# Feed-forward's first product by seven half products (Strassen) in place of eight for 20 of 22 pairs of tiles; adaLN's pace 0.2 for 0.25

## The chip, the cores and the metric

The kernel runs on one core of a Trainium2 chip. The metric is the device time of one execution in microseconds (us), as the median of three runs. The engines are named as in the profile: PE multiplies matrices (PEld is its weight load), DVE is the vector engine, ACT the scalar engine, POOL the GpSimd engine, and SP issues the loads.

## The reference

Two layers of a trunk run for 512 latent and 128 context tokens, 640 tokens in all, with weights shared between both groups. What matters here is the second half of each layer and the modulation vectors that it needs:

```python
def _adaln(cvec, w, b):
    m = jnp.dot(jax.nn.silu(cvec), w) + b          # w: 1024 x 6144
    return jnp.split(m, 6, axis=-1)

def _swiglu(h, w1, w2):                             # h: 640 x 1024
    a = jnp.dot(h, w1)                              # w1: 1024 x 5632
    gt, up = jnp.split(a, 2, axis=-1)
    return jnp.dot(jax.nn.silu(gt) * up, w2)        # w2: 2816 x 1024

# in each of the two layers, after the four mixers and their merge
xp = xp + gt2 * _swiglu(_modulate(_rmsnorm(xp, norm2_g[l]), sh2, sc2), w_ffn_in[l], w_ffn_out[l])
xs = xs + gt2 * _swiglu(_modulate(_rmsnorm(xs, norm2_g[l]), sh2, sc2), w_ffn_in[l], w_ffn_out[l])
```

## The kernel before

Every product is made in three passes: each fp32 operand x is held as a rounded part hi and a rest lo = x - hi, and `mm3` (L406 to L408) adds hi by hi, hi by lo and lo by hi in PSUM. A weight tile of 128 x 1024 values is loaded in one transfer of 512 KB into one of two `raw` buffers; `wload` then copies each half of 512 columns to `whi` on ACT (L394) and subtracts on DVE to get `wlo` (L395). There are five `whi` and five `wlo` buffers of 512 columns in turn, so a half can be made up to five halves ahead. These instructions carry a high priority for the scheduler (`WPRI`), and so do the evacuations (`EPRI`).

The normalised activations stand as `hT`, eight k-tiles of hi and lo for 640 tokens. Feed-forward's first product runs over 22 pairs j of weight tiles, a gate tile and an up tile of 128 columns of w1. Each tile takes 8 k-tiles x 3 passes for two groups of tokens, 256 and 384 (`GROUPS`): 48 matmuls a tile, 96 a pair. The gate's PSUM goes through Silu on ACT (L1768), DVE multiplies the up's PSUM by it (L1771), and `split` (L443 on ACT, L444 on DVE) makes hi and lo of the result. The pairs come in groups of 6, 6, 6 and 4 (`FF_SPLIT`), and after each group the second product adds its share to the residual: 20 tiles of 256 columns a group, `t` on DVE (L1623) and the addition to `big` on POOL for three quarters of them (L1624). The activations of the groups stand in turn in the buffers `kv` and `m` with `q`.

Beside this runs adaLN in the background (`adaln_all`), in slices of 512 columns: per step one tile `wm` of w_mod is loaded, DVE adds its product with the one vector into `msum0` (L471, a SCALAR_TENSOR_TENSOR), and ACT (L465) and POOL (L467) do the same for the other into `mtmp` and `msum1`. Eight steps make a slice; PE then transposes the sums (L478) and DVE reduces them (L479). `tick()` is called once per stretch of matmuls, and each call adds `BGRATE` steps. At four places of a layer `bg_until` emits what is still missing.

The Tile scheduler decides the order in which each engine's instructions stand, by its own estimate of when operands are ready. On the chip each engine then works through its list in that order.

Of the kernel before, what the change touches and what calls it, by code (L numbers as in the profile page):

```python
# [78 lines left out]
FF_SPLIT = (6, 6, 6, 4)  # L79

WPRI = 20000
EPRI = 500
DEFER = 2
BGRATE = 0.25
W3 = 1
# [136 lines left out]
def trunk(ctx: ExitStack, tc: tile.TileContext, a: dict, depth: int):  # L222
# [103 lines left out]
    ofs = Slots("of", 4, NTOK)  # L326
    raw_ring = ring("raw", 2, [P, 1088])
    hi_ring = ring("whi", 5, [P, 544], F32R)
# [154 lines left out]
    def adaln_all(items):  # L483
# [9 lines left out]
        for i, (l, ch) in enumerate(items):  # L493
# [6 lines left out]
            if (ch // 2) % 3 == 2:  # L500
# [5 lines left out]
                yield True  # L506
                ps = acc()
                T.transpose(ps[:8, :P], gcol, ident)
# [1176 lines left out]
    def mixers(l, d, *start):  # L1685
# [30 lines left out]
        drive(bulk, streams)  # L1716

    def layer(l, *start):
        d = {"of": {}, "m": [], "mg": []}
# [25 lines left out]
        if l + 1 < depth:  # L1745
            smalls(l + 1)
        j0 = 0
        for g, cnt in enumerate(FF_SPLIT):
            acts = []

            def fo(n, bufs=None):
                return sum((wload(l, ("fo", g, n, k), bufs=bufs) for k in range(0, cnt, 4)), [])
            for jx in range(cnt):
                j = j0 + jx
                if g == 3 and jx == 1:

                    extra = [ks.take(F32R) for _ in range(4)]
                    bufs = [(t[:, 0:512], t[:, 512:1024]) for t in extra]
                    pieces = {2: fo(2, bufs)}
                if g == 3 and jx == 2:  # L1760
                    pieces[3] = fo(3, bufs)
                pl = ks if g % 2 == 0 else (ms if jx < 4 else qs)
                sl = pl.take(F32R)
                at = r32(sl).rearrange("p (w n) -> p w n", w=2)
                sg = f640()

# [8 lines left out]
                for groups in (LATE, EARLY) if j == 0 else (GROUPS,):  # L1775
# [4 lines left out]
                    run(fm(wu, KT, hmov, cb, groups))  # L1780
                acts.append((at, pl, sl))
            if g == 0:
                gts = gate_rows(l, 1)
            if g == 3:
                if l + 1 < depth:
# [10 lines left out]
            else:  # L1796
                pieces = {0: fo(0), 1: fo(1), **pieces}
                hook = norm_tm(xs, pieces, cnt, lhs, gts, ks, 0 if l + 1 < depth else None)
                ks.give(*extra)
            for at, pl, sl in acts:  # L1800
# [9 lines left out]
    def final(x, ss, tt):  # L1810
        out = qs.take()
        qs.give(out)
        r = norm_r(ss)
# [87 lines left out]
```

## Time and profile before

| | |
|---|---|
| median of 3 runs | 2796.37 us (2795.75 to 2799.54) |
| profiled execution, its own time | 2797.74 us |
| its span | 2796.0 us |
| mean granted TensorE clock | 0.994 |
| PE busy | 2727.5 us, 98% of the span |
| DVE busy | 1853.6 us, 66% |
| ACT busy | 1352.5 us, 48% |
| POOL busy | 520.4 us, 19% |

A share of 98% means that PE is hardly ever without an instruction in flight; the shares of the others are means over stages that differ. Feed-forward runs from about 954 to 1420 us in the first layer and from about 2330 us to the end in the second.

### The profile page before, as it was taken

The page shows a single profiled execution, that of the slowest core. Times are in us where ns is not written, and L with a number is a line of the kernel's source. Part 1 is how long each engine was busy: PE and PEld are TensorE (multiplying, and loading weights), DVE is VectorE, ACT ScalarE, POOL GpSimd, SP SyncE. Part 2 cuts the span into 40 slices and gives each one's busy share as a digit, 9 for nine tenths or more (in the row PEclk, how much of TensorE's full clock was granted, in tenths as well). Part 3 has the DMA queues.
Part 4 walks back from the last instruction along what each step waited for, and adds up shares of the span by engine and source line. Part 5 has one row for each costly group of instructions (what it writes and reads, how often), then busy time and mean ns, then how long its engine had stood idle before and what let it go on. Part 6 is the DMA issues. An engine that isn't in the chain of part 4 may idle for free.

```text
span 2796.0 us, 51577 instructions
## 1 busy us (share of the span) xinstructions
PE 2727.5 (98%) x19946; PEld 2679.6 (96%) x19946; DVE 1853.6 (66%) x4412; ACT 1352.5 (48%) x3122; POOL 520.4 (19%) x506
## 2 busy tenths in 40 slices
PE   7999999999999999999989999999999999999998
PEld 4999999999999999999989989999999999999998
DVE  7786768888984746455587776888888445334344
ACT  5865446656653533233358654456666334222222
POOL 2010222120233404223150001211100221101012
PEclk9999999999999999999999999999999999999999
DMA  7233323121234324233332233211111232222221
GB/s 284 89 102 101 106 94 97 48 77 63 76 117 145 98 81 130 94 118 99 129 118 91 94 118 110 80 61 46 49 62 62 82 121 76 76 76 76 73 99 64
DMA packets 113206, 264.26 MB, mean 95 GB/s; under 512 B 13040, under 2 KB 38992, under 8 KB 112960
## 3 DMA queue, kind: packets, MB, share of 16 engines
q1 hardware_dynamic: 112960, 260.97, 28.6%
q8 instruction: 156, 2.56, 0.4%
q14 instruction: 90, 0.74, 0.1%
HBM read 252.73 MB, written 7.95 MB: 93 GB/s over the span
## 4 chain that ended last, share of the span: by engine, by line
PE 82%; DVE 9%; ACT 3%; issue 2%; DMA 2%; POOL 1%; SPq 0%; DVEq 0%; POOLq 0%; ACTq 0%
PE acc L406 23%; PE acc L407 23%; PE acc L408 23%; PE O L1216 2%; PE T L1206 2%; DVE msum L471 2%; DVE wlo L395 1%; DMA raw<-wflat 1%; PE S L1173 1%; DMA wm<-w_mod 1%; PE S L1174 1%; PE T L942 1%; ACT whi L394 1%; PE S L1473 0%; PE S L1182 0%
## 5 line engine op out<-in xcount | busy, mean ns | idle before, releaser
L406 PE MATMUL acc<-hT,whi 128*128 128x256 f32 (+1 forms) x3392 | 1053.9, 312 | 19.5 <-DVE hT L661 5.1
L407 PE MATMUL acc<-hT,whi 128*128 128x256 f32 (+1 forms) x3392 | 1054.3, 311 | 4.4 <-DVE hT L604 1.8
L408 PE MATMUL acc<-hT,wlo 128*128 128x256 f32 (+1 forms) x3392 | 1050.3, 310 | 0.1
L395 DVE TENSOR_TENSOR wlo<-raw,whi 128x512 fp32r<-128x512 f32 (+1 forms) x632 | 475.7, 757 | 366.0 <-ACT whi L394 363.6
L394 ACT CAST whi<-raw 128x512 fp32r<-128x512 f32 (+1 forms) x632 | 388.8, 620 | 626.8 <-PE acc L407 394.7
L406 PEld LDWEIGHTS acc<-hT,whi 128*128 128x128 f32 x3392 | 640.9, 189 | 26.7 <-DVE hT L661 5.9
L407 PEld LDWEIGHTS acc<-hT,whi 128*128 128x128 f32 x3392 | 642.2, 189 | 7.6 <-DVE hT L604 2.5
L408 PEld LDWEIGHTS acc<-hT,wlo 128*128 128x128 f32 x3392 | 641.3, 189 | 1.1 <-DVE wlo L395 0.4
L467 POOL TENSOR_TENSOR msum<-msum,mtmp 128x512 f32<-128x512 f32 x140 | 206.6, 1476 | 387.3 <-ACT msum L465 269.9
L1624 POOL TENSOR_TENSOR big<-big,t 128x256 f32<-128x256 f32 x150 | 125.6, 843 | 660.5 <-DVE t L1623 653.1
L1596 POOL TENSOR_TENSOR m<-m,f 128x256 f32<-128x256 f32 x96 | 98.0, 1023 | 558.0 <-DVE f L1594 343.7
L406 PE MATMUL acc<-whi,kv 128*128 128x256 f32 x660 | 183.8, 281 | 2.3 <-DVE t L1623 2.3
L408 PE MATMUL acc<-whi,kv 128*128 128x256 f32 x660 | 183.6, 281 | 0.0
L407 PE MATMUL acc<-wlo,kv 128*128 128x256 f32 x660 | 183.3, 281 | 0.0
L1623 DVE TENSOR_TENSOR t<-acc,P 128x256 f32<-128x256 f32 x200 | 83.7, 421 | 126.3 <-PE acc L408 108.0
L721 ACT CAST pth<-T 128x512 fp32r<-128x512 f32 (+1 forms) x232 | 117.9, 522 | 96.9 <-PE T L1206 38.2
L406 PE MATMUL acc<-big,whi 128*128 128x256 f32 (+1 forms) x512 | 158.9, 310 | 3.5 <-ACT f L1588 3.5
L465 ACT ACTIVATE mtmp<-wm,csil 128x512 f32<-128x512 f32 x140 | 101.1, 722 | 121.8 <-POOL msum L467 109.1
L407 PE MATMUL acc<-big,whi 128*128 128x256 f32 (+1 forms) x512 | 158.8, 310 | 0.0
L408 PE MATMUL acc<-big,wlo 128*128 128x256 f32 (+1 forms) x512 | 158.4, 310 | 0.0
L722 DVE TENSOR_TENSOR ptl<-T,pth 128x512 fp32r<-128x512 f32 (+1 forms) x232 | 137.4, 602 | 31.2 <-ACT pth L721 30.1
L471 DVE SCALAR_TENSOR_TENSOR msum<-wm,csil,msum 128x512 f32<-128x512 f32 x140 | 148.2, 1059 | 7.4 <-DMA wm<-w_mod 6.2
(400 smaller groups left out, 5447.2 us busy)
## 6 DMA issues: line engine op xcount, KB each, us to landing
raw<-wflat SPq DMA_DIRECT2D x308, 512.0 KB
wm<-w_mod SPq DMA_DIRECT2D x160, 256.0 KB
kv<-nbias SPq DMA_DIRECT2D x16, 576.0 KB
raw<-wflat SPq DMA_DIRECT2D x24, 256.0 KB
kv<-mdr SPq DMA_DIRECT2D x16, 320.0 KB
big<-x_sample SPq DMA_DIRECT2D x8, 512.0 KB
P<-gt_d SPq DMA_DIRECT2D x32, 128.0 KB
kv<-w_mod SPq DMA_DIRECT2D x12, 256.0 KB
```

What stands on the lines that cost most here:

```text
L394: S.copy(hi[:, :n], raw[:, s0:s0 + n])
L395: V.tensor_tensor(lo[:, :n], raw[:, s0:s0 + n], hi[:, :n].bitcast(F32), ALU.subtract)
L406: T.matmul(ps, lhs(k, 0), rhs(k, 0), start=(k == 0), stop=False)
L407: T.matmul(ps, lhs(k, 0), rhs(k, 1), start=False, stop=False)
L408: T.matmul(ps, lhs(k, 1), rhs(k, 0), start=False, stop=(k == kn - 1))
L465: S.activation(accs[v][:, :512] if kk == 0 else tmp, w, AF.Copy, scale=s)
L467: G.tensor_tensor(accs[v][:, :512], accs[v][:, :512], tmp, ALU.add)
L471: V.scalar_tensor_tensor(accs[v][:, :512], w, s, accs[v][:, :512], ALU.mult, ALU.add)
L721: S.copy(hi[:, :n], ps[:, :n])
L722: V.tensor_tensor(lo[:, :n], ps[:, :n], hi[:, :n].bitcast(F32), ALU.subtract)
L1596: G.tensor_tensor(mt[:, c0:c0 + n], mt[:, c0:c0 + n], gate[:, c0:c0 + n], ALU.add)
L1624: (V if n == 3 else G).tensor_tensor(xs[tt][:, 256 * n:256 * n + 256], xs[tt][:, 256 * n:256 * n + 256], t[:, :256], ALU.add)
```

## The change

For pairs 2 to 21 of each layer, the gate and up tiles and the 640 tokens are seen as 2 x 2 blocks: two halves of k (512 each), two tiles (gate, up) and two halves of the tokens (320 each). Strassen's scheme in Winograd's form then takes seven products of 4 k-tiles x 3 passes x 320 tokens, 84 matmuls a pair, in place of eight. In return sums are made: of the activations once per layer (`ff_sums`: S2, S3, S4 into six `kv` buffers, S1 over the second token half of `hT`'s first four k-tiles), of the weights for each pair (`ff_load`: t1 to t4, all on POOL), and of the products (`ff_pair`: the u's and y's, from PSUM, on DVE). All seven weight operands are split into hi and lo, before it was four halves. The first two pairs (`FF_PLAIN`) stay as they were, and the sums of the activations are made meanwhile. The four quarter tiles of a pair are loaded by four transfers of 256 KB into six half buffers in place of two of 512 KB into two buffers. All groups keep their activations in `m` and `q`. A pair has 4 ticks in place of 8, and `BGRATE` is 0.2. The gate rows' transpose goes to a `T` buffer of PSUM in place of an `acc` one.

```diff
+FF_PLAIN = 2
+HALF = 320
...
-BGRATE = 0.25
+BGRATE = 0.2
...
-                ps = acc()
+                ps = bT()
                 T.transpose(ps[:8, :P], gcol, ident)
...
+    def ff_sums(held, s1):
+        sop = [[r32(held[2 * i + x]).rearrange("p (k w n) -> p k w n", k=2, w=2) for x in range(2)] for i in range(3)]
+        for k in range(4):
+            x = [p640().rearrange("p (h n) -> p h n", h=2) for _ in range(2)]
+            for i, c0 in enumerate((0, HALF)):
+                hi, lo = [hT[:, k:k + 5:4, w, c0:c0 + HALF].bitcast(F32) for w in range(2)]
+                (V if i and k % 2 == 0 else G).tensor_tensor(x[i], hi, lo, ALU.add)
...
+            V.tensor_tensor(t1, a21, a22, ALU.add)
+            V.tensor_tensor(s2, t1, a11, ALU.subtract)
+            V.tensor_tensor(s3, a11, a21, ALU.subtract)
+            V.tensor_tensor(a12, a12, s2, ALU.subtract)
+            for i, t in enumerate((s2, s3, a12)):
+                o = sop[i][k // 2][:, k % 2]
+                split(o[:, 0], o[:, 1], t)
+            yield
...
+            b11, b12, b22, b21 = half(2 * j, 0), half(2 * j + 1, 0), half(2 * j + 1, 1), half(2 * j, 1)
+            t1, t2, t3, t4 = [t[:, :512] for t in ts]
+            G.tensor_tensor(t1, b12, b11, ALU.subtract)
+            G.tensor_tensor(t2, b22, t1, ALU.subtract)
+            G.tensor_tensor(t3, b22, b12, ALU.subtract)
+            G.tensor_tensor(t4, b21, t2, ALU.subtract)
+        for x in (b11, t2, t3, t1, b21, t4, b22):
+            with tc.high_priority(offset=WPRI):
+                hi, lo = hi_ring()[:, :512], lo_ring()[:, :512]
+                split(hi, lo, x)
+            yield hi, lo
...
+        prod(pa, "A11", True)
+            S.copy(u3, pa)
+        prod(pb, "S2", True)
+            V.tensor_tensor(u2, pb, u3, ALU.add)
+        yield
+        prod(pc, "S3", True)
+            V.tensor_tensor(u3, pc, u2, ALU.add)
+        prod(pd, "S1", True)
+            V.tensor_tensor(y[:, h2], pd, u3, ALU.add)
+        yield
+        prod(pa, "A12", False)
+            S.activation(x[:, h1], pa, AF.Silu)
+        prod(pc, "A22", False)
+            V.tensor_tensor(x[:, h2], pc, u2, ALU.add)
+            S.activation(x[:, h2], x[:, h2], AF.Silu)
+        yield
+        out(h2)
+        prod(pd, "S4", False)
+            V.tensor_tensor(y[:, h1], pd, u2, ALU.add)
+        out(h1)
+        yield
...
-                pl = ks if g % 2 == 0 else (ms if jx < 4 else qs)
+                pl = ms if jx < 4 else qs
...
+                if j >= FF_PLAIN:
+                    run(ff_pair(ops, ff_load(l, j, spare, ts), at))
+                    continue
...
+                next(sums, None)
+                next(sums, None)
+                if j == FF_PLAIN - 1:
+                    for _ in sums:
+                        pass
+                    for k in range(4):
+                        split(hT[:, k, 0, HALF:], hT[:, k, 1, HALF:], s1[:, HALF * k:HALF * k + HALF])
```

The lists below show where the changed instructions stand. The changed kernel's lines are eight or more higher: its L452 is the subtraction of `split` (L444 before), its L479, L477 and L487 are adaLN's on DVE (L471, L469, L479 before), its L475 is adaLN's on POOL (L467 before). `wlo` with a number is one of the five buffers of weight rests, `of` are the weight sums t1 to t4, `raw` and `q_24` the half buffers of loaded weights.

DVE's list in the first layer's first group, around one plain pair before:

```order
L395 TENSOR_TENSOR wlo_145<-raw_137,whi_140 128x512
L1771 TENSOR_TENSOR f_152<-acc_162,f_152 128x256
L444 TENSOR_TENSOR kv_49_10332<-f_152,kv_49_10332 128x256
L395 TENSOR_TENSOR wlo_146<-raw_137,whi_141 128x512
L1771 TENSOR_TENSOR f_152<-acc_163,f_152 128x384
L395 TENSOR_TENSOR wlo_147<-raw_136,whi_142 128x512
L444 TENSOR_TENSOR kv_49_10332<-f_152,kv_49_10332 128x384
```

The same engine in the same group of the changed kernel, part of the second Strassen pair:

```order
L452 TENSOR_TENSOR wlo_144<-of_30_10000,whi_139 128x512
L1824 TENSOR_TENSOR f_153<-O_169,f_151 128x320
L487 TENSOR_REDUCE modr<-T_167 128x4
L452 TENSOR_TENSOR wlo_145<-of_31_10001,whi_140 128x512
L479 SCALAR_TENSOR_TENSOR msum_69<-wm_68,csil,msum_69 128x512
L1831 TENSOR_TENSOR f_152<-acc_164,f_151 128x320
L626 TENSOR_TENSOR modc<-modr,sm 128x8
L452 TENSOR_TENSOR wlo_146<-of_29_9999,whi_141 128x512
L479 SCALAR_TENSOR_TENSOR msum_69<-wm_65,csil,msum_69 128x512
L452 TENSOR_TENSOR wlo_143<-of_32_10002,whi_138 128x512
L1809 TENSOR_TENSOR f_152<-f_152,f_153 128x320
L479 SCALAR_TENSOR_TENSOR msum_69<-wm_66,csil,msum_69 128x512
```

Between the weight rests that PE needs next there now stand evacuations of products and steps of adaLN; in the other three groups of the layer no step of adaLN stands between the pairs.

POOL's list at the same place of the changed kernel (before, it held nothing there between the last addition to `hT` and the second product but five of adaLN's additions):

```order
L1770 TENSOR_TENSOR of_29_9999<-q_24_9998,raw_137 128x512
L475 TENSOR_TENSOR msum_70<-msum_70,mtmp 128x512
L1771 TENSOR_TENSOR of_30_10000<-q_24_9998,of_29_9999 128x512
L1773 TENSOR_TENSOR of_32_10002<-raw_136,of_30_10000 128x512
L475 TENSOR_TENSOR msum_70<-msum_70,mtmp 128x512
L1772 TENSOR_TENSOR of_31_10001<-raw_137 128x512
```

The weight sums of a pair and adaLN's additions follow each other there without another kind of work between them.

## Rows read from the trace of the kernel before

**Rows 1.** Page, busy time of each engine, its share of the span and instructions.

```profile
PE 2727.5 (98%) x19946; PEld 2679.6 (96%) x19946; DVE 1853.6 (66%) x4412; ACT 1352.5 (48%) x3122; POOL 520.4 (19%) x506
```

**Rows 2.** Windows: length, PE, PEld, DVE, ACT, POOL busy, then PE's clock and DMA.

```profile
80.00:955.00 875.00, 857.82 (x6292) 844.01 (x6291) 673.88 (x1741) 501.58 (x1191) 174.39 (x160) 1.00 0.29 92
955.00:995.00 40.00, 38.12 (x260) 37.48 (x259) 28.29 (x37) 17.77 (x34) 12.51 (x9) 0.96 0.38 121
...
1425.00:2320.00 895.00, 874.55 (x6414) 865.73 (x6413) 654.41 (x1740) 500.82 (x1221) 140.68 (x140) 0.99 0.26 84
2405.00:2490.00 85.00, 85.00 (x655) 85.00 (x654) 34.10 (x63) 20.40 (x37) 12.14 (x15) 1.00 0.24 77
2490.00:2530.00 40.00, 40.00 (x280) 40.00 (x279) 13.38 (x23) 12.15 (x23) 0.00 (x0) 1.00 0.22 73
```

**Rows 3.** Timeline of ACT, one gate tile's first Silu and that five pairs later.

```profile
2454.38 0.39 ACT L1768 ACTIVATE f<-acc 128x256 f32<-128x256 f32 x1 [2.10 <-PE acc L408]
...
2523.69 0.39 ACT L1768 ACTIVATE f<-acc 128x256 f32<-128x256 f32 x1 [1.62 <-PE acc L408]
```

**Rows 4.** Timeline of PE: start, duration; matmuls of 384, 256 and 320 columns.

```profile
2400.81 0.33 PE L408 MATMUL acc<-hT,wlo 128*128 128x384 f32 x1
2400.98 0.34 PE L406 MATMUL acc<-hT,whi 128*128 128x384 f32 x1
...
2500.30 0.28 PE L406 MATMUL acc<-hT,whi 128*128 128x256 f32 x1
2500.41 0.28 PE L407 MATMUL acc<-hT,whi 128*128 128x256 f32 x1
...
519.83 0.31 PE L1173 MATMUL S<-kv,q 128*128 128x320 f32 x1
519.97 0.31 PE L1174 MATMUL S<-kv,q 128*128 128x320 f32 x1
```

**Rows 5.** DVE by line and shape in 2490:2530: count, busy us, mean ns.

```profile
L395 DVE TENSOR_TENSOR wlo<-raw,whi 128x512 fp32r<-128x512 f32 x12 | 8.3, 693 | 19.1 <-ACT whi L394 19.1
L1771 DVE TENSOR_TENSOR f<-acc,f 128x384 f32<-128x384 f32 x3 | 1.7, 558 | 2.6 <-PE acc L408 2.6
...
L1771 DVE TENSOR_TENSOR f<-acc,f 128x256 f32<-128x256 f32 x2 | 0.9, 426 | 3.1 <-PE acc L408 3.1
```

**Rows 6.** Timeline of DVE and POOL, a second product's residual.

```profile
2409.72 0.69 DVE L395 TENSOR_TENSOR wlo<-raw,whi 128x512 fp32r<-128x512 f32 x1
2410.33 0.55 DVE L444 TENSOR_TENSOR kv<-f,kv 128x384 fp32r<-128x384 f32 x1
...
2420.23 1.82 DVE L395 TENSOR_TENSOR wlo<-raw,whi 128x512 fp32r<-128x512 f32 x2
...
2418.26 0.73 POOL L1624 TENSOR_TENSOR big<-big,t 128x256 f32<-128x256 f32 x1 [1.39 <-DVE t L1623]
2420.39 1.11 POOL L1624 TENSOR_TENSOR big<-big,t 128x256 f32<-128x256 f32 x1 [1.39 <-DVE t L1623]
```

**Rows 7.** Timeline of DVE and POOL, adaLN's steps in the first layer's feed-forward.

```profile
960.41 1.50 DVE L661 CAST hT<-t 128x512 fp32r<-128x512 f32 x1
961.84 0.74 DVE L471 SCALAR_TENSOR_TENSOR msum<-wm,csil,msum 128x512 f32<-128x512 f32 x1
962.50 1.78 DVE L395 TENSOR_TENSOR wlo<-raw,whi 128x512 fp32r<-128x512 f32 x1
...
1054.38 0.41 DVE L1623 TENSOR_TENSOR t<-acc,P 128x256 f32<-128x256 f32 x1
1054.71 1.43 DVE L471 SCALAR_TENSOR_TENSOR msum<-wm,csil,msum 128x512 f32<-128x512 f32 x1
...
1054.08 1.51 POOL L467 TENSOR_TENSOR msum<-msum,mtmp 128x512 f32<-128x512 f32 x1 [0.84 <-ACT mtmp L465]
...
1057.84 1.29 POOL L467 TENSOR_TENSOR msum<-msum,mtmp 128x512 f32<-128x512 f32 x1
1059.09 0.73 POOL L1624 TENSOR_TENSOR big<-big,t 128x256 f32<-128x256 f32 x1
```

**Rows 8.** What PE waited for in 945:1425: us, times, longest.

```profile
PE acc L406 <- DVE t L1623: 3.5, 4, 1.3
PE acc L407 <- POOL hT L662: 1.2, 1, 1.2
PE acc L406 <- DVE hT L661: 0.6, 1, 0.6
```

**Rows 9.** Windows of PE: length, busy, granted clock, DMA.

```profile
962.00:964.00 2.00, 0.80 (x4) 0.99 0.21 31
964.00:966.00 2.00, 2.00 (x11) 0.50 0.59 178
966.00:968.00 2.00, 2.00 (x13) 0.65 0.61 208
```

More of the change, by code (lines that the diff above doesn't have):

```diff
@@ L326, in trunk, with raw_ring @@
     ofs = Slots("of", 4, NTOK)
-    raw_ring = ring("raw", 2, [P, 1088])
+    raw_tiles = [cp.tile([P, 1088], F32, name=f"raw{i}") for i in range(2)]
+    raw_at = [0]
+    def raw_ring():
+        raw_at[0] += 1
+        return raw_tiles[raw_at[0] % 2]
     hi_ring = ring("whi", 5, [P, 544], F32R)
@@ new lines, in ff_ops, with ff_load, half @@
+    def ff_ops(held):
+        sop = [[r32(held[2 * i + x]).rearrange("p (k w n) -> p k w n", k=2, w=2) for x in range(2)] for i in range(3)]
+        ops = {"S" + str(i + 2): lambda k, w, o=o: o[k // 2][:, k % 2, w] for i, o in enumerate(sop)}
+        ops["A11"] = lambda k, w: hT[:, k, w, :HALF]
+        ops["A12"] = lambda k, w: hT[:, 4 + k, w, :HALF]
+        ops["A22"] = lambda k, w: hT[:, 4 + k, w, HALF:]
+        ops["S1"] = lambda k, w: hT[:, k, w, HALF:]
+        return ops
+    def ff_load(l, j, spare, ts):
+        parts = ff_halves(spare)
+        with tc.high_priority(offset=WPRI):
+            def half(tile, h):
+                off, x = PLAN[("fi", tile)]
+                t = parts()
+                SY.dma_start(t, a["wflat"][l, off:off + P * x].rearrange("(p x) -> p x", p=P)[:, 512 * h:512 * h + 512])
+                return t
+            b11, b12, b22, b21 = half(2 * j, 0), half(2 * j + 1, 0), half(2 * j + 1, 1), half(2 * j, 1)
[5 more added lines that the diff above has]
+        for x in (b11, t2, t3, t1, b21, t4, b22):
+            with tc.high_priority(offset=WPRI):
+                hi, lo = hi_ring()[:, :512], lo_ring()[:, :512]
+                split(hi, lo, x)
+            yield hi, lo
@@ L1747, in layer @@
         j0 = 0
+        held, s1, spare = [ks.take(F32R) for _ in range(6)], qs.take(), qs.take()
+        ts = [ofs.take() for _ in range(4)]
+        ops = ff_ops(held)
+        sums = ff_sums(held, s1)
         for g, cnt in enumerate(FF_SPLIT):
@@ L1755, in layer @@
                 if g == 3 and jx == 1:
-                    extra = [ks.take(F32R) for _ in range(4)]
+                    extra = [qs.take(F32R) for _ in range(2)]
                     bufs = [(t[:, 0:512], t[:, 512:1024]) for t in extra]
@@ L1780, in layer @@
                     run(fm(wu, KT, hmov, cb, groups))
-                acts.append((at, pl, sl))
+                next(sums, None)
[3 more added lines that the diff above has]
+                        pass
+                    for k in range(4):
+                        split(hT[:, k, 0, HALF:], hT[:, k, 1, HALF:], s1[:, HALF * k:HALF * k + HALF])
+                    qs.give(s1)
             if g == 0:
@@ L1784, in layer @@
             if g == 3:
+                ks.give(*held)
+                qs.give(spare)
+                ofs.give(*ts)
                 if l + 1 < depth:
@@ L1810, in final @@
     def final(x, ss, tt):
-        out = qs.take()
-        qs.give(out)
+        out = ks.take()
+        ks.give(out)
         r = norm_r(ss)
```

38 lines of the change are left out of this document (37 added, 1 removed).

## The prediction

> **What bounds the kernel now.** I read the page's busy times first [rows 1]: PE 98% of the span, the others far below. Then the windows, since such shares are means [rows 2]: between 2405 and 2530 us, in the second layer's feed-forward, PE is busy without a gap while DVE is at a third and POOL at nothing or a seventh. So work taken from PE there shortens the kernel, as long as the other engines keep up with the faster pair. The first layer differs: in 955:995 PE is idle for 1.9 us, POOL is busy for 12.5 of 40, and PE waits for `hT` from DVE and POOL [rows 2, 8]. That is the place to look at, because the change puts its new work just there. DVE and POOL may not be costed by their busy time alone. In [rows 6] a subtraction of 512 columns takes 0.69 us (0.61 from start to start), but two of them in a row take 1.82 us while POOL makes one addition, which itself takes 1.11 in place of 0.73: 0.61 + 0.73 + 0.61 is about that, so they ran one after the other. The same holds for a cast that takes 1.50 us, a subtraction with 1.78 and a step of adaLN with 1.43 beside POOL's additions, whereas an evacuation from PSUM in the middle of such an addition takes its usual 0.41 [rows 7].
>
> **PE's saving.** One pair now takes (2523.69 - 2454.38)/5 = 13.86 us [rows 3], which over 96 matmuls is 144.4 ns each, a mean of 114 for 256 columns and 174 for 384; two of 320 columns elsewhere start 140 ns apart [rows 4]. I take 144.4 ns for 320, in the middle of 256 and 384. A Strassen pair of 84 matmuls is then 12.13 us, 1.73 us less, and 40 pairs save 69.3 us. The Trainium skill ("TensorE: Matmul & The Clock Gate", section "Back-to-back issue gap") gives columns / 2.4 + 2.5 ns for isolated matmuls at the higher clock; that would make 13.04 and 11.41 us of the pairs and 65 us of the saving, an estimate by that page. The rows are slower than it by 5 to 7%, and the sum goes by the rows.
>
> **The new work in a pair.** DVE makes seven weight rests (0.61 us start to start), four operations of 320 columns between SBUF operands (two products, two rests: 0.49 from between 256 and 384 [rows 5], less the same 0.08 of overlap, 0.41) and five that read PSUM (0.41). POOL makes four weight sums of 512 columns (1.25 start to start [rows 7]). One after the other, what excludes each other is 5.9 + 5.0 = 10.9 us, and the PSUM operations are 2.05 more: 12.13 us is just enough if they lie beside POOL's sums, and a pair would take 12.95 if they never did. In the list, DVE's operations from PSUM wait for PE, POOL fills such gaps, and a weight is prepared four products (7 us) ahead, so I take PE's 12.13 with 0.1 us on each of the 32 pairs outside the first groups: 3 us. The bounds are 0 and 0.82 x 32 = 26 us. The Trainium skill ("SBUF — State Buffer", section "Who interferes with whom") says that a DVE instruction with two SBUF inputs and a POOL instruction that reads SBUF block each other whole, and that DVE with one SBUF input is free of it. By that page the lower bound can be reached, without exclusion at all DVE would need 7.95 of 12.13 us; the trace agrees on both halves (1.82 and 0.41 us above).
>
> **The first group of the first layer.** Here the order decides. From the evacuation of the last transposed norm tile to the last weight rest of the group's sixth pair, DVE's list holds 33 operations of 512 columns with two SBUF operands (20.1 us at 0.61), 24 steps of adaLN (15.8 at 0.66 [rows 7]), 8 casts or scalings (3.2 at 0.4), 42 of 320 columns (17.2) and five others (2.4): 58.7 us. POOL's list holds 16 weight sums, 19 additions of adaLN and two parts of `hT` (46.3 at 1.25), six sums over 640 columns (1.57 each in proportion, 9.4) and a small one: 56.3 us. Together 115.0 us that exclude each other. PE's work meanwhile is 22 matmuls of 384 (3.8), the early token group of pair 0 (5.4), pair 1 (13.9) and four Strassen pairs but for the last product (46.8): 69.9 us. PE must wait for 45 us. Before, the list had 8 adaLN steps in the whole group, and PE waited for 1.9 us. The reason for the 24 is the pace: at 0.2 a step, and 4 ticks a pair, adaLN is behind when feed-forward begins (92 products done against 100), and the scheduler has brought all that it owes in this layer into this one group.
>
> **The first group of the second layer.** There adaLN is done. From the same point to the last rest of the activations' sums S2 and S3, DVE's list holds 20.5 us by the same prices and POOL's 17.5 (six sums of 640, four weight sums, two parts of `hT`): 38.0 us. PE has 27 matmuls of 384, 48 of 256, pair 1 and 40 matmuls of 320: 29.8 us. It waits for 8.2 us. The rest of the group is below PE's time.
>
> **What else moves.** The two places' own waits of now go: 1.2 + 0.6 for `hT`, 3.5 behind the background burst in the second product [rows 8], and half of the 3 us at half clock after them [rows 9], 7 us. The exclusion is not used without a gap: 4% of 153 us, 6 us. The mixers get 16 more of adaLN's steps (56 in the second layer for 32, 8 fewer in the first). All of PE's idle time there is 17.2 + 20.5 us [rows 2]; if 96 steps made all of it, a step costs 0.4 us, so 0 to 6 us, and I take 5. The four transfers in place of two move the same bytes and are issued a pair ahead; `m` and `q` for every group's activations cost nothing, since PE has read a group's before the next pair ends; the gate transpose in another PSUM buffer neither. A group's last half result needs about 3 us behind the last product (four DVE operations and a cast), and the second product has 30 matmuls of 256 (3.4 us) of the first five k-tiles before it: nothing.
>
> **The sum**, against the profiled execution's 2797.7 us: - 69.3 + 45 + 8.2 - 7 + 6 + 3 + 5 = 2788.6. That execution is 1.4 us above the median, so 2787 us, 0.3% faster.
>
> **Rivals.** (a) DVE and POOL hide more than I count, so that most of the saving stays. For it: 24 of the first group's operations are not needed by a product. Against it: each engine takes its list in order. If the first layer waited only as long as the second (8), it would be 2750; with no wait at all 2728. (b) The other sign: the steady pair is bound by DVE and POOL in turn. Its place is the groups 2 to 4 of both layers, its price up to 26 us in place of 3, 2810; against the 2796 of now it decides from 0.4 us a pair on. For it: 12.95 is above 12.13, and POOL's t1 to t4 depend on each other. (c) PE's waits bring its clock down. In [rows 9], after 0.80 us of work in 2, it is granted 0.50 and 0.65 for 4 us, that is 1.2 GHz for about 3. In the first layer's first group PE would have 70 us of work in 115. If it ran wholly at 1.2 GHz its work were 140, and 25 us come on top: 2812. Against it: a slow PE does not wait and so regains its clock; a third of it, 8 us, makes no change out of the gain. (d) The Strassen pairs are not 1/8 shorter on PE, because weights load behind smaller matmuls; the 140 ns in [rows 4] speak against it.
>
> **How the numbers follow.** My case as worked out 0.50, with its own range of 2773 to 2803; (a) 0.20; (b) 0.18; (c) 0.10; (d) 0.02. What a measurement of this kernel can tell from no change is 0.2%, 5.6 us. Of my case 0.30 lies below 2790.8, 0.15 within 5.6 us of 2796.4 and 0.05 above; (a) is faster; (b) and (c) are slower for 0.22 and the same for 0.06, (d) is slower. That gives 0.50 faster, 0.21 the same, 0.29 slower. The range 2755 to 2816 leaves out the far half of (a) and the ends of (b) and (c).
>
> **What would show it.** In the profile after: two Silu rows of one kind a pair apart by 12.1 us in the second layer's second group (right), 12.5 or more with DVE busy nearly all the time (rival b). In the first layer's first group PE busy for only some 60% over 115 to 120 us, waiting for `wlo` and for the activations' sums, with DVE's subtractions at 1 to 2 us beside POOL; the granted clock there says how much of (c) there is. In the second layer's first group a wait of some 10 us before or in pair 2, none later. The second products at 41 us a group as now. The prediction is wrong if PE is busy through the first layer's first group, if a pair's steady distance is not near 12.1, or if the mixers move by more than 10 us.

## The result, and the profile after

The changed kernel takes 2817.3 us in the median of five runs (2814.16 to 2824.26), the kernel before 2796.37 on the same chip (2793.17 to 2800.61): a ratio of 1.0077, with an interval of 1.0056 to 1.0098. It is slower by 0.8%. 2787 us and a gain had been forecast, with 2816 as the upper end. The profiled execution took 2822.84 us, 5.5 above its median; its span is 2821.0 us, 25.0 more than that of before.

The page after, busy times, and TensorE's granted clock in 40 slices of the span:

```profile
PE 2701.9 (96%) x19466; PEld 2642.6 (94%) x19466; DVE 2175.1 (77%) x4800; ACT 1440.7 (51%) x3314; POOL 782.8 (28%) x678
...
PEclk9999999999999889999999999999999999999999
```

Against [rows 1] PE has 26 us less of busy time, with 69.3 us of work taken away, and DVE and POOL have 322 and 262 us more. The clock row dips in the two slices from 917 to 1058 us, which hold the end of the output projection and most of layer 1's first group.

For the table, the span is cut where the first `t` of a residual and the first Silu of a group stand in the trace. A group's row holds the second product of the group ahead of it, the first group's row doesn't. "Ahead of feed-forward" is all up to the output projection. The third and fourth columns are the first two experiments below.

| us | before | changed | before, pace 0.2 | before, T bank |
|---|---|---|---|---|
| layer 1, ahead of feed-forward | 892.7 | 891.9 | 901.4 | 881.2 |
| output projection and norm | 59.7 | 70.8 | 70.8 | 59.6 |
| group 1 | 85.8 | 131.5 | 89.4 | 85.0 |
| group 2 | 128.6 | 117.6 | 126.5 | 128.6 |
| group 3 | 128.6 | 117.7 | 130.1 | 128.5 |
| group 4 | 103.3 | 100.3 | 100.0 | 103.0 |
| layer 2, all ahead of feed-forward | 931.0 | 936.8 | 939.0 | 930.4 |
| group 1 | 81.6 | 92.9 | 82.0 | 81.6 |
| groups 2 and 3 | 251.1 | 232.6 | 251.1 | 251.1 |
| group 4 | 99.7 | 95.2 | 99.7 | 99.7 |
| last residual | 33.8 | 33.7 | 33.8 | 33.8 |

So the middle groups give what they should, 40.4 us in all (those of layer 1 also lost 25 of their 32 steps of adaLN), and six stages give it back: both first groups (+45.7 and +11.3), the output projection (+11.1), what lies ahead of layer 2's feed-forward (+5.8), and the last groups by saving 7.5 in place of 13.8.

Two windows of before that [rows 2] doesn't have, the output projection and layer 1's first group (in these and the next the numbers are the window, its length, busy time of PE, PEld, DVE, ACT and POOL, then PE's clock and the DMA):

```profile
892.70:952.40 59.70, 59.70 (x495) 59.65 (x494) 36.59 (x83) 26.44 (x71) 19.62 (x23) 1.00 0.34 111
952.40:1038.20 85.80, 83.92 (x580) 83.25 (x579) 44.73 (x66) 33.45 (x63) 13.60 (x9) 0.98 0.29 93
```

The windows after that answer to them and to [rows 2], here cut at the stages: the output projection, layer 1's first group and the pairs of its second and fourth group; then layer 2's first group and the pairs of its second and fourth.

```profile
891.90:962.60 70.70, 65.13 (x510) 64.41 (x509) 49.20 (x96) 30.96 (x77) 30.61 (x30) 0.95 0.36 116
962.60:1094.10 131.50, 99.76 (x588) 92.92 (x586) 129.00 (x169) 61.76 (x120) 81.04 (x52) 0.87 0.37 115
1141.60:1211.70 70.10, 70.10 (x492) 70.10 (x492) 61.05 (x90) 33.24 (x67) 23.64 (x16) 1.00 0.28 87
1375.30:1429.70 54.40, 48.67 (x309) 47.01 (x307) 41.08 (x62) 23.21 (x47) 16.72 (x11) 0.94 0.29 91
...
2366.50:2459.40 92.90, 84.64 (x567) 81.82 (x565) 80.95 (x129) 41.78 (x87) 35.92 (x23) 0.96 0.26 81
2505.30:2575.70 70.40, 70.40 (x496) 70.40 (x494) 61.14 (x90) 33.58 (x67) 23.98 (x16) 1.00 0.30 93
2740.30:2787.30 47.00, 42.70 (x294) 41.58 (x292) 38.87 (x60) 21.14 (x44) 13.37 (x9) 1.00 0.26 85
```

In layer 1's first group DVE is busy for 129.0 of 131.5 us and PE for 99.8: there DVE, slowed by POOL as the next timeline shows, is the bound. In the middle groups PE is busy without a gap, DVE for 87% and POOL for a third.

The steady pair, the timeline of ACT in layer 2's second group, one kind of Silu and the same five pairs later:

```profile
2505.30 0.43 ACT L1828 ACTIVATE f<-acc 128x320 f32<-128x320 f32 x1
...
2566.53 0.43 ACT L1828 ACTIVATE f<-acc 128x320 f32<-128x320 f32 x1
```

A pair takes (2566.53 - 2505.30)/5 = 12.25 us, where [rows 3] gave 13.86.

How DVE and POOL stand beside each other in layer 1's first group, a timeline as in [rows 6, 7]:

```profile
1031.88 0.68 DVE L452 TENSOR_TENSOR wlo<-raw,whi 128x512 fp32r<-128x512 f32 x1
1032.48 1.77 DVE L479 SCALAR_TENSOR_TENSOR msum<-wm,csil,msum 128x512 f32<-128x512 f32 x1
1034.18 1.75 DVE L452 TENSOR_TENSOR wlo<-of,whi 128x512 fp32r<-128x512 f32 x1
1035.86 0.48 DVE L1831 TENSOR_TENSOR f<-acc,f 128x320 f32<-128x320 f32 x1
...
1038.38 0.47 DVE L1837 TENSOR_TENSOR f<-O,f 128x320 f32<-128x320 f32 x1
...
1031.96 1.75 POOL L1772 TENSOR_TENSOR of<-q 128x512 f32<-128x512 f32 x1 [3.27 <-DVE msum L479]
1033.67 1.71 POOL L475 TENSOR_TENSOR msum<-msum,mtmp 128x512 f32<-128x512 f32 x1
...
1038.13 1.47 POOL L1770 TENSOR_TENSOR of<-q,raw 128x512 f32<-128x512 f32 x1 [0.64 <-DVE wlo L452]
```

The first weight rest, begun just before POOL's sum, takes its usual 0.68 us and the sum 1.75. Each operation after it begins while POOL is busy: the step of adaLN takes 1.77, the next weight rest 1.75, and POOL's addition 1.71. This is what [rows 6] showed. The evacuation from PSUM at 1038.38 lies wholly inside a POOL sum and takes its usual 0.47. Over the whole group, DVE by shape (count, busy us, mean ns):

```profile
L479 DVE SCALAR_TENSOR_TENSOR msum<-wm,csil,msum 128x512 f32<-128x512 f32 x28 | 31.4, 1122 | 0.1
L452 DVE TENSOR_TENSOR wlo<-of,whi 128x512 fp32r<-128x512 f32 x16 | 16.6, 1041 | 0.3 <-ACT whi L451 0.3
L403 DVE TENSOR_TENSOR wlo<-raw,whi 128x512 fp32r<-128x512 f32 x8 | 10.6, 1332 | 1.1 <-ACT whi L402 1.1
...
L477 DVE TENSOR_SCALAR msum<-wm,csil 128x512 f32<-128x512 f32 x5 | 3.6, 713 | 0.0
```

33 steps of adaLN stand in this group (L479 and L477), where the trace of before has 8, and the operations of 512 columns with two operands in SBUF that are shown here take 1.04 to 1.33 us in the mean, 1.5 to 1.9 times the 0.68 to 0.74 that they take alone in [rows 6, 7] and at 1031.88. DVE hardly idles ahead of any of them: it is a queue that is full.

What PE waited for in the output projection, where before it was busy for all of the 59.70 us:

```profile
PE acc L415 <- DVE hT L670: 3.1, 1, 3.1
PE acc L414 <- DVE hT L669: 2.5, 1, 2.5
```

It waits for the normalised activations, which DVE and POOL make. 8 steps of adaLN stand in this stage now, none before. In layer 1's first group the waits are spread over what DVE and ACT deliver, of which the four longest kinds are these:

```profile
PE acc L1803 <- ACT hT L451: 6.2, 1, 6.2
PE acc L414 <- DVE hT L669: 3.3, 1, 3.3
PE acc L1804 <- DVE kv L452: 3.0, 1, 3.0
PE acc L414 <- ACT f L1900: 2.8, 1, 2.8
```

### The profile page after: what moved, and what is told of

It is laid out like the page before. It is cut to its first block, busy times and chain, and to the rows that moved or that the text cites. A ratio compares the mean times of both kernels' runs of the same rounds, so it can differ in the third digit from the quotient of the medians.

```text
span 2821.0 us, 51942 instructions
## 1 busy us (share of the span) xinstructions
PE 2701.9 (96%) x19466; PEld 2642.6 (94%) x19466; DVE 2175.1 (77%) x4800; ACT 1440.7 (51%) x3314; POOL 782.8 (28%) x678
## 4 chain that ended last, share of the span: by engine, by line
PE 74%; DVE 14%; ACT 5%; issue 3%; DMA 2%; POOL 1%; SPq 0%; DVEq 0%; POOLq 0%; ACTq 0%
PE acc L414 16%; PE acc L415 16%; PE acc L416 16%; PE acc L1803 3%; PE acc L1805 3%; PE acc L1804 3%; PE O L1224 2%; PE T L1214 2%; DVE msum L479 2%; DVE wlo L403 2%; DVE wlo L452 1%; DMA raw<-wflat 1%; PE O L1803 1%; PE O L1804 1%; PE O L1805 1%
## 5 line engine op out<-in xcount | busy, mean ns | idle before, releaser
L414 PE MATMUL acc<-hT,whi 128*128 128x256 f32 (+1 forms) x2112 | 667.0, 318 | 28.1 <-DVE hT L669 10.5
L415 PE MATMUL acc<-hT,whi 128*128 128x256 f32 (+1 forms) x2112 | 666.1, 316 | 6.0 <-DVE hT L670 4.5
L416 PE MATMUL acc<-hT,wlo 128*128 128x256 f32 (+1 forms) x2112 | 662.7, 314 | 1.0 <-DVE wlo L403 1.0
L402 ACT CAST whi<-raw 128x512 fp32r<-128x512 f32 (+1 forms) x472 | 289.4, 619 | 436.6 <-PE acc L415 172.8
L403 DVE TENSOR_TENSOR wlo<-raw,whi 128x512 fp32r<-128x512 f32 (+1 forms) x472 | 358.2, 764 | 145.9 <-ACT whi L402 135.1
L414 PEld LDWEIGHTS acc<-hT,whi 128*128 128x128 f32 x2112 | 404.2, 192 | 35.1 <-DVE hT L669 11.4
L415 PEld LDWEIGHTS acc<-hT,whi 128*128 128x128 f32 x2112 | 405.3, 192 | 9.5 <-DVE hT L670 5.7
L416 PEld LDWEIGHTS acc<-hT,wlo 128*128 128x128 f32 x2112 | 404.6, 192 | 2.1 <-DVE wlo L403 1.1
L475 POOL TENSOR_TENSOR msum<-msum,mtmp 128x512 f32<-128x512 f32 x140 | 210.9, 1507 | 267.8 <-ACT msum L473 153.9
L451 ACT CAST whi<-of 128x512 fp32r<-128x512 f32 x160 | 98.8, 619 | 134.7 <-PE acc L1804 54.8
L1803 PE MATMUL acc<-hT,whi 128*128 128x320 f32 x480 | 152.1, 317 | 13.5 <-DVE f L1821 8.8
L414 PE MATMUL acc<-whi,m 128*128 128x256 f32 x560 | 158.2, 284 | 5.2 <-DVE t L1631 5.1
L415 PE MATMUL acc<-wlo,m 128*128 128x256 f32 x560 | 157.8, 282 | 0.2 <-DVE wlo L403 0.2
L416 PE MATMUL acc<-whi,m 128*128 128x256 f32 x560 | 157.2, 281 | 0.0
```

The source lines that it names most:

```text
L402: S.copy(hi[:, :n], raw[:, s0:s0 + n])
L403: V.tensor_tensor(lo[:, :n], raw[:, s0:s0 + n], hi[:, :n].bitcast(F32), ALU.subtract)
L414: T.matmul(ps, lhs(k, 0), rhs(k, 0), start=(k == 0), stop=False)
L415: T.matmul(ps, lhs(k, 0), rhs(k, 1), start=False, stop=False)
L416: T.matmul(ps, lhs(k, 1), rhs(k, 0), start=False, stop=(k == kn - 1))
L475: G.tensor_tensor(accs[v][:, :512], accs[v][:, :512], tmp, ALU.add)
```

## The experiments

The theory to begin with (A): DVE's and POOL's work in SBUF excludes each other, and the first and last groups hold more of it than PE's time. The rivals: the pace is the main cause (B), DVE's own time without exclusion is (C), and others as they came up. Counts of adaLN's steps below are DVE's instructions in the trace of the run named, within the stages of the table.

**The pace alone**, in the kernel before.

```diff
-BGRATE = 0.25
+BGRATE = 0.2
```

> The kernel before with adaLN's pace 0.2 and nothing else. Theory A (VectorE's and GpSimd's work in SBUF exclude one another, and the first and last groups hold more of it than TensorE's time): the plain groups have room for a few adaLN steps more (VectorE 44.7 us and GpSimd 13.6 us of 85.8 us in the first group of layer 1), so the time stays within 4 us of the kernel before, 2793 to 2801 us. Rival B (the pace is the main cause, by the steps that are forced at the gate rows and by a worse order in the mixers): the mixers grow by some 10 us in layer 1 and 6 us in layer 2 as in the changed kernel, 2808 to 2816 us.

2822.87 us, ratio 1.0085 (1.0063 to 1.0106). Without any Strassen pair, the pace alone makes the kernel as slow as the whole change does. Theory A's part on the plain groups holds (the four of layer 1 take 446.0 us for 446.3 in all, though the first takes 89.4 for 85.8), but its time does not. The costs are where B put them, and larger (its range ended at 2816): 8.7 us ahead of the output projection, 11.1 in it, 8.0 ahead of layer 2's feed-forward. Ahead of the projection 16 steps of adaLN fewer stand than before (84 for 100), so those 8.7 us are not the price of steps; their cause was not found. The window of the projection reads as in the changed kernel, with 8 steps of adaLN in it:

```profile
901.40:972.20 70.80, 65.32 (x513) 64.47 (x512) 48.65 (x94) 31.01 (x77) 30.41 (x30) 0.95 0.34 113
```

**One PSUM bank alone**, in the kernel before.

```diff
-                ps = acc()
+                ps = bT()
                 T.transpose(ps[:8, :P], gcol, ident)
```

> The kernel before with one line of the change: the transposes of adaLN's gate columns go to the T bank of PSUM in place of one of the three acc banks. The changed kernel spent 10 to 12 us less ahead of the feed-forward of layer 1 than the kernel before at the same pace (891.9 against 901.4 us at 0.2, 880.2 against 892.7 us at 0.25, up to the first residual). Theory A: that comes from this line, since an acc bank no longer waits for adaLN; 2783 to 2791 us. Rival F (it comes from a shift of the schedule that the rest of the change brings): 2796 to 2803 us.

2783.46 us, ratio 0.9946 (0.993 to 0.9963): 15 us faster, as theory A had it. This line of the change is a gain of its own, and it hid the pace's cost in the mixers of layer 1 (901.4 with the pace, 881.2 with the bank, 891.9 with both). Between 80 us and the output projection PE is idle for 9.3 us in place of 17.2; which of its waits the bank had caused is not shown.

**The changed kernel with the pace of before.**

```diff
-BGRATE = 0.2
+BGRATE = 0.25
```

> The changed kernel with the pace back at 0.25. In VectorE's order 28 of adaLN's steps still stand within the first group of layer 1 (32 in the changed kernel), none is forced. Theory A: the first group of layer 1 stays within 6 us of its 131.5 us, the last group of layer 1 loses up to 8 us of its 61.4 us (7 forced steps fewer), in all 2805 to 2817 us. Rival B (the pace is the main cause): the mixers' 16 us come back and the first group falls by 20 us or more, 2775 to 2790 us.

2800.64 us, ratio 1.0005 (0.9996 to 1.0014): no difference from before, and between the ranges of both theories. Each had half of it. The output projection is back at 59.6 us with no step of adaLN in it, and the part ahead at 880.2. The first group of layer 1 stays at 130.8 us, with 31 steps of adaLN for 33, so they stand there whatever the pace; and its last group did not change (100.4), so the seven steps forced behind it cost nothing. Ahead of layer 2's feed-forward it still takes 936.3 us for 931.0 before, with 48 steps for 32, since a Strassen pair has half the ticks at either pace: that cost is not shown to be the pace's.

```profile
939.80:1070.60 130.80, 100.12 (x590) 93.97 (x588) 126.93 (x168) 60.45 (x115) 77.23 (x48) 0.84 0.35 109
```

**adaLN held back from layer 1's first group.** At the pace of 0.25, the list gets a dependence without a semaphore, so that the scheduler may not bring adaLN's later steps forward into this group; behind it adaLN goes on at 0.3 a tick.

```diff
+            if l == 0 and g == 0:
+                bg_until(0, 10, 11)
+                bg[0] = 0.0
...
+            if l == 0 and g == 0:
+                held_off.append(list(nc.cur_bb.bb.instructions)[-1])
+                bg[0] = 0.3
...
+                        after(ins, held_off[0], "adaLN behind the first group")
```

> The changed kernel at the pace 0.25 with adaLN's steps held back from the first group of layer 1: no step stands in it (28 without the hold), and after it they come at 0.3 a yield; the order then puts 24 steps into the six pairs of the second group. Theory A: the first group falls from 130.8 us to 80 to 95 us, since adaLN's work is what VectorE and GpSimd cannot do beside the rest; the second group grows from 70.1 us by 10 to 30 us, since its pairs have little room: 2765 to 2785 us. Rival G (the sums of activations and weights alone fill the first group, adaLN only takes time that is idle): the first group stays over 115 us, 2790 to 2805 us.

2802.86 us, ratio 1.0021 (1.0012 to 1.003). The time lies in rival G's range, but G had the first group over 115 us: it falls from 130.8 to 98.2 us (theory A had 80 to 95) with 4 steps in its window for 31, 1.2 us a step. The second grows from 118.6 to 145.1 with 23 steps in its pairs for none, 1.15 us a step, which gives most of it back. The last group grows from 100.4 to 112.8 with 8 steps in its pairs. The two windows, then the steps and POOL's additions in the second:

```profile
939.20:1037.40 98.20, 86.74 (x566) 84.58 (x564) 86.11 (x129) 44.88 (x91) 39.76 (x26) 0.91 0.26 82
1085.80:1182.50 96.70, 79.82 (x519) 77.45 (x517) 91.94 (x126) 45.45 (x87) 50.34 (x33) 0.93 0.39 121
```

```profile
L476 POOL TENSOR_TENSOR msum<-msum,mtmp 128x512 f32<-128x512 f32 x17 | 26.1, 1535 | 29.8 <-ACT msum L474 21.6 <-ACT mtmp L474 8.2
L480 DVE SCALAR_TENSOR_TENSOR msum<-wm,csil,msum 128x512 f32<-128x512 f32 x20 | 22.5, 1126 | 0.4 <-DMA wm<-w_mod 0.4
```

So steady Strassen pairs have little room for adaLN: a step taken out of one group is paid for in the next at the same price. By the prediction's prices a step is 0.66 us on DVE and 1.25 on POOL, 1.9 one after the other, so about a third of it did find room.

**The sums on DVE**, first in the changed kernel, then in the run that holds adaLN back.

```diff
-            G.tensor_tensor(t1, b12, b11, ALU.subtract)
+            V.tensor_tensor(t1, b12, b11, ALU.subtract)
...
-                (V if i and k % 2 == 0 else G).tensor_tensor(x[i], hi, lo, ALU.add)
+                V.tensor_tensor(x[i], hi, lo, ALU.add)
```

> The changed kernel with the four sums of weights of each pair, and the six sums over 640 columns, on VectorE in place of GpSimd. Theory A: each such sum excludes the other engine for some 0.61 us in place of 1.25, so the first group of layer 1 falls by some 15 us, that of layer 2 by 8 us, the last groups by 3 to 5 us each, and the steady pairs stay at 12.3 us: 2780 to 2795 us. Rival C (VectorE's own time is the bound, without exclusion): VectorE has 20 sums of 0.61 us more in the first groups, which it fills already: 10 to 13 us longer in each, 2825 to 2845 us.

2804.81 us, ratio 1.0018 (1.0009 to 1.0028), between the two. Layer 1's first group grows by 4.6 us to 136.1, but the scheduler put 38 steps of adaLN there for 33, so this run doesn't tell the theories apart in that place. At 1.2 us a step the five more are 6 us, which leaves a gain of 1 to 2 us by the sums (an estimate), where theory A had 15. In layer 2, without adaLN, the first group falls from 92.9 to 89.2 us and the last from 95.2 to 89.8.

> The run with adaLN held back from the first group of layer 1 (two plain pairs, pace 0.25), with the sums of weights and the six sums over 640 columns on VectorE in place of GpSimd. No adaLN stands in the first group in either, so this is the sums alone. Theory A (exclusion): 22 sums at half the time take 10 to 15 us off the first group, 98.2 to 83 to 88 us; the last groups lose 4 to 6 us each: 2775 to 2792 us. Rival C (VectorE's own time): the first group grows to 105 us or more, 2805 to 2820 us.

2777.96 us, ratio 0.993 (0.9915 to 0.9944). The time is within theory A's range, by luck in part: 20 of the 28 us between the profiles of the two runs come from layer 1's last group (112.8 to 92.7), out of which the order took its 16 steps of adaLN. The first group has 4 steps in both and falls from 98.2 to 92.9 us, where A had 83 to 88; that of layer 2 falls from 93.6 to 86.9. That is 5 to 7 us, half of what exclusion alone was to give. C, which had the first group at 105 or more, is out. One rival stays: a sum also takes half as long on DVE (0.61 us for 1.25), and t2 waits for t1 and t4 for t2, so a shorter chain of sums could give these 5 to 7 us without any exclusion; no run separates the two. Some 14 us over the 78.9 that the first group would take (85.8 less four pairs of 1.73) remain with POOL nearly idle, and DVE at 84%. The window, then PE's longest wait in it:

```profile
941.10:1034.00 92.90, 85.60 (x566) 83.36 (x564) 78.48 (x151) 45.05 (x91) 5.50 (x4) 0.94 0.28 88
...
PE O L1808 <- ACT hT L452: 1.9, 1, 1.9
```

PE is idle for 7.3 us of this group, 5.4 more than before, and busy for 85.6, which is 8.6 more than before's 83.9 less the 6.9 saved, at a mean clock of 0.94 for 0.98.

**Four plain pairs first in place of two**, at the pace 0.2, then at 0.25, then with adaLN held back.

```diff
-FF_PLAIN = 2
+FF_PLAIN = 4
...
                 next(sums, None)
-                next(sums, None)
```

(A plain pair then makes one step of the activations' sums in place of two, so that they spread over the four.)

> The changed kernel with four plain pairs at the start of each layer in place of two, so 18 Strassen pairs of 22 (the sums are spread over four pairs, one yield each). In VectorE's order 8 of adaLN's steps stand within the first group of layer 1 in place of 32. It gives up two pairs a layer, 2 x 2 x 1.73 = 6.9 us. Theory A: the first group's wait in layer 1 falls from some 52 us to under 15 us, that in layer 2 to under 4 us, the other groups stay: 2775 to 2790 us. Rival E (the crowding only moves to the groups behind, since the same adaLN steps must run there): the second to fourth groups of layer 1 grow by what the first loses, 2815 to 2825 us.

2767.09 us, ratio 0.989 (0.9873 to 0.9906), below theory A's range. The first group has 8 steps of adaLN for 33 and takes 94.7 us for 131.5; that of layer 2 takes 85.4 for 92.9, though two of its pairs are now longer. Nothing came up in the groups behind (118.3, 118.9 and 97.8 us for 117.6, 117.7 and 100.3), so rival E is out.

> Four plain pairs first, as in the run before, with the pace at 0.25. Theory A: the output projection of layer 1 comes back from 70.8 to 59.7 us and the part ahead of it falls by some 6 to 10 us, the first group grows by up to 8 us since 8 of adaLN's steps stand in it as before: 2748 to 2760 us. Rival B' (the pace does not matter where the first group is plain): 2764 to 2770 us.

2757.12 us, ratio 0.9854 (0.984 to 0.9869), within theory A's range. The projection and the mixers are back at 59.6 and 879.7 us. The second group grew from 118.3 to 127.9, with 12 steps of adaLN in its pairs for none, 0.8 us a step.

> Four plain pairs first, pace 0.25, and adaLN's steps held back from the first group of layer 1 as in the run above; 24 of them then stand in the second group. Theory A: the first group falls to 84 to 90 us, the second grows by 10 to 30 us; in all no better than four plain pairs at 0.25 without the hold, 2752 to 2775 us. Rival H (the steady pairs have room for adaLN): the second group stays within 3 us of 70.7 us, 2738 to 2750 us.

2768.53 us, ratio 0.9894 (0.9879 to 0.9909): against the run before it the first group falls to 86.5 us, with 4 steps for 8, and the second rises to 139.7, with 20 steps in its pairs for 12. Rival H is out.

**Two paces**: 0.25 up to layer 1's feed-forward and 0.2 from there to the end, the mixers of layer 2 among it, with four plain pairs.

```diff
         for g, cnt in enumerate(FF_SPLIT):
             acts = []
+            bg[0] = 0.2
```

> Four plain pairs first, adaLN's pace 0.25 in the mixers and 0.2 in feed-forward. In VectorE's order no step of adaLN stands between the Strassen pairs of layer 1 (16 of them stand beside or in the second group at 0.25 throughout, of which 8 between its pairs). Theory A (a step between steady Strassen pairs costs all of its time, a step beside plain pairs or second products nothing): the second group falls from 79.3 us to 70 to 71 us, all else stays: 2745 to 2752 us. Rival H (the steady pairs have room): 2754 to 2760 us, the time at 0.25 throughout.

2749.58 us, ratio 0.9828 (0.9813 to 0.9843), with the run after it the fastest here: 1.7% faster than before, and within theory A's range. Its windows are the projection, the first group and the pairs of the second:

```profile
880.10:939.70 59.60, 59.60 (x494) 59.57 (x493) 36.84 (x82) 26.50 (x71) 19.61 (x23) 1.00 0.32 103
939.70:1033.30 93.60, 85.51 (x593) 84.50 (x591) 76.85 (x117) 43.09 (x87) 37.64 (x24) 0.96 0.34 105
1081.60:1152.30 70.70, 70.70 (x498) 70.70 (x497) 62.42 (x91) 33.38 (x67) 24.73 (x17) 1.00 0.30 92
```

The same steps stand beside the second products now, 8 in each of three, and cost nothing that shows.

> The run with two paces, with the four sums of weights on VectorE in place of GpSimd in the last group of each layer alone. Theory A (a sum excludes the other engine for 1.25 us on GpSimd and 0.61 us on VectorE): the last group of layer 2 falls from some 43.8 us to 41 to 43 us; in that of layer 1 the order now puts 8 steps of adaLN between the pairs, which cost 0 to 12 us: 2743 to 2760 us. Rival C (VectorE's own time is the bound): the last group of layer 2 grows by 2 to 5 us.

(The engine of t1 to t4 is chosen by `j >= 18`.) 2750.02 us, ratio 0.9831 (0.9817 to 0.9846). Layer 2's last group falls by 0.9 us only, to 89.9, less than theory A had and not the growth that C had; layer 1's grows from 96.2 to 103.3 with 8 steps of adaLN in its pairs for 2.

> The run with two paces, with five plain pairs first in place of four. It gives up 1.73 us in each layer. Theory A: with one Strassen pair in the first groups the waits there (some 11 and 7 us with four plain pairs) fall by another 2 to 6 us each: 2740 to 2750 us, within 5 us of four plain pairs.

(`FF_PLAIN = 5`.) 2764.97 us, ratio 0.988 (0.9863 to 0.9896): a miss. The first groups did not fall (94.8 and 86.7 us for 93.6 and 85.3), so the fifth plain pair buys nothing, and the last groups rose from 96.2 to 112.6 and from 90.8 to 95.5. In the last groups of layer 2, which have no adaLN, two and five plain pairs give the same 95.2 to 95.5 us and four give 90.6 to 91.0. What two and five share there is the turn of the six half buffers: the last group begins at the same one.

**The turn of the half buffers**, shifted by 4 with two plain pairs at 0.25, and by 2 in the run with two paces.

```diff
         ts = [ofs.take() for _ in range(4)]
+        half_at[0] += 4
```

> The changed kernel at the pace 0.25 with the turn of the six half buffers shifted by four, so that the last group of each layer begins at the same buffer as with four plain pairs. The last group also loads four tiles of the second product's weights into the two raw buffers that hold four of the six halves. Theory P (in the last group a weight sum waits for a transfer because a half and such a tile meet in one buffer): the last group falls from 54.5 to 45 to 49 us in layer 1 and from 47.3 to 43 to 45 us in layer 2, with nothing else changed but some 36 for 31 steps of adaLN in the first group of layer 1: 2785 to 2800 us. Rival Q (it comes from the number of plain pairs or from adaLN): the last groups stay within 1 us.

2791.03 us, ratio 0.9976 (0.9967 to 0.9986), 0.3% less than the 1.0005 without the shift, each against the kernel before on its own chip. The last group of layer 1 falls from 100.4 to 91.1 us and that of layer 2 from 95.5 to 92.0, though layer 1's first group got 35 steps of adaLN for 31 and rose to 137.7. What waits in layer 1's last group, first without the shift, then with it (total us, times, longest):

```profile
POOL of L1770 <- DMA raw<-wflat: 19.7, 2, 10.3
ACT m L451 <- DVE f L1809: 8.6, 7, 4.0
ACT whi L451 <- DMA raw<-wflat: 5.2, 2, 3.4
```

```profile
ACT m L451 <- DVE f L1809: 6.1, 5, 2.7
POOL of L1770 <- DMA raw<-wflat: 4.5, 1, 4.5
```

> The run with two paces (four plain pairs) with the turn of the six half buffers shifted by two, so that the last group begins at the buffer of the changed kernel. Theory P: the last group of layer 2 rises from 43.9 to 47 us; that of layer 1, where the order now also puts 8 steps of adaLN between the pairs, from 46.5 to some 64 us as with five plain pairs: 2762 to 2772 us. Rival Q: the last group of layer 2 stays at 43.9 us.

2763.88 us, ratio 0.9882 (0.9865 to 0.9898): layer 2's last group rises from 90.8 to 95.3 us, layer 1's, with 8 steps of adaLN in its pairs for 2, from 96.2 to 112.9. Theory P holds in both directions. In this group the weights of the second product's last columns pass through the `raw` buffers, four of the six halves lie in the same two, and at the wrong turn a weight sum of layer 1 waits 10 us for its transfer. In layer 2's last group POOL's longest wait without the shift is 9.2 us and is put down to a weight rest on DVE; that chain was not followed, so there the turn is shown as the cause, but not the way in which it acts.

## Why the prediction was wrong

**The saving and the steady pair: right.** 12.23 us a pair was forecast and 12.25 measured. The four middle groups gave 40.4 us where 24 pairs by 1.63 are 39.1. Rival (b) did not come. That DVE and POOL have little room left in such a pair (10.9 us that exclude each other) holds too: the steps pushed into the second group cost 1.15 us each.

**What else moves: the step that failed first.** The prediction gave the mixers "0 to 6 us, and I take 5". Ahead of the two feed-forwards, 16.1 us were added (-0.8, +11.1, +5.8), and that is net of a gain of 12 us by the T bank in layer 1 (11.5 in that run's profile), which the prediction had as nothing. The pace alone costs 19.8 us ahead of layer 1's feed-forward and 8.0 ahead of layer 2's. The prediction had named this as what would make it wrong: mixers that move by more than 10 us. The working was a mean price over 96 steps that had found idle engines; the question was where the displaced slice would land. It landed in the output projection's end, where the norm's tail on DVE and POOL stands directly ahead of PE, and the stage took 70.7 to 70.8 us in all four runs with 8 steps in it and 59.6 to 59.7 in all others, which have none. That pays for 11.1 of the 16.1 us. For the other 5 no cause is shown: with the pace back the changed kernel still took 936.3 us ahead of layer 2's feed-forward, and over the kernels with Strassen pairs this stage lies between 929.1 and 941.5 us without following its number of steps (40 to 61).

**The first group of layer 1: right in kind, wrong in its reason, a little small.** By its terms the stage was to grow by 39 us (45 of wait and 4.6 of gaps, less 6.9 saved and 3.3 of its own old waits); it grew by 45.7. DVE busy for 98% of the stage and the pairs of 1.7 us in the timeline are the exclusion that was costed; how much of the stage it makes up is not shown, since moving the sums off POOL gave half of what it was to give, or less. PE was busy for 76% of the stage, where some 60% had been named: it idled for 31.7 us, and was busy for 22.8 more than before's 83.9 less the 6.9 saved, at a mean clock of 0.87. But "the reason for the 24 is the pace" fell: at 0.25 there are 31 steps in place of 33. The scheduler brings them forward into this group at either pace, by its own estimate of idle time on DVE. With four plain pairs first it brings 8. The hold shows that 27 of those steps are worth 32.6 us; what the sums cost on their own is about 19 (98.2 for 78.9). The forecast had no such split.

**The first group of layer 2: too small.** It was to grow by about 3 us (8.2 of wait and its gaps, less 6.9) and grew by 11.3. PE idled for 8.3 us, so the wait was as long as forecast; but PE was busy for 84.6 us, some 10 more than before's 81.2 less 6.9, and for that the sum had no term. There is no adaLN there, and the sums on DVE take 4 to 7 us of it off, so exclusion or the shorter chain is some of it. "The rest of the group is below PE's time" is what the forecast said after pair 2; how much of the remainder is the sums' order in DVE's list and how much PE's lower clock (0.96 there) was not separated.

**The last groups: not in the sum.** They saved 3.0 and 4.5 us for the 6.9 each that the saving contains. The prediction let the four transfers cost nothing because they carry the same bytes and are issued a pair ahead. In the last group they share their buffers with other loads, and that cost 9 and 3.5 us by the turn alone.

**Rival (c), the clock,** is in the rows: where [rows 9] had it low for some 4 us, its mean is 0.87 over layer 1's whole first group, and 0.91 with adaLN held back. Since DVE is busy for nearly all of that group, PE's lower clock need not have cost anything there. With the sums on DVE and adaLN held back, DVE leaves 16% of that group free and the clock is at 0.94, so it may have cost some of the 8.6 us by which PE is busy longer; no run took it apart.

So the sum missed by 34 us: 11 ahead of feed-forward, 6 and 9 in the first groups, 6 in the last groups, and the rest in small terms. Without the pace the change would have been neither faster nor slower (2800.64 against 2799.53 us), and with the turn shifted as well it is 0.2% faster. The T bank is in that, and gives 0.5% by itself: the Strassen pairs alone would then be some 0.6% slower than before (1.0005 / 0.9946, an estimate; no run has them alone).

## What to carry to other kernels

A constant that paces background work is a change of its own: cost it by asking which stage the displaced slice lands in and whether that stage has idle time on the same engines, not by a mean price per step. Where PE's work is shortened by giving more to two other engines, count what excludes each other against the new, shorter time, and expect that the spare time which used to absorb background work is gone: here a step of adaLN went from 0.1 us to 0.8 to 1.2. (The 0.1 is an estimate: before, the pairs of a middle group took 83.4 us with 8 steps in layer 1 and 82.5 with none in layer 2.) And where buffers of two users overlap, the point of the turn at which they meet is worth a look at the transfers that end late.

## What had not been expected of the hardware

The exclusion was as large as read before, and selective: 1.77 and 1.75 us beside POOL for 0.68 alone, but 0.47 for an evacuation from PSUM inside a POOL sum. The Trainium skill ("SBUF — State Buffer", section "Who interferes with whom") has DVE with two SBUF inputs and POOL block each other, and the timeline agrees. The prediction's short form, that one SBUF input is free of it, holds for the evacuations that it was used for; the section excepts DVE's 2-port modes, and the cast of [rows 7], with one SBUF input, took 1.50 us beside POOL. What was not expected is how little the removal gave: with POOL busy for 5.5 of 92.9 us, the group lost 5.3 us. At 84%, DVE is not the bound of that group by its time alone, and PE still waited; whether the order of DVE's list, ACT's part or PE's clock holds the rest was not separated.
